# Two matrix products on one core, each done by seven half-sized block products in place of eight

## The chip, the cores and the metric

One core of one Trainium2 chip. The metric is the device time of the program in microseconds (us); lower is better. Executions of one kernel agree here to about 0.2%.

## The reference

```python
batch, m, k, h, n = 16, 512, 768, 3072, 768       # all inputs float32
y = np.matmul(x, w1) + b1                         # (8192 x 768) @ (768 x 3072)
y = 0.5 * y * (1.0 + erf(y / np.sqrt(2.0)))       # Gelu
return np.matmul(y, w2)                           # (8192 x 3072) @ (3072 x 768)
```

Both products have the same number of multiplications. I call them product one and product two.

## The kernel before

Everything is cast to fp16 by the loads. W1 and W2 stay in SBUF. Rows are taken in blocks of 512, and the scheduler orders the engines.

```python
for mb in range(n_mblk):                                  # 16 blocks of 512 rows
    gT = gtp.tile([P, HC, MB], F16, name="gT")
    for hc in range(HC):                                  # product one: 24 groups of 6 matmuls
        py = ps_y.tile([P, MB], FP32, ...)
        for kc in range(KC):
            nc.tensor.matmul(out=py[:], lhsT=w1b[:, kc, hc*P:(hc+1)*P], rhs=xT_cur[:, kc, :], ...)
        nc.scalar.activation(out=gT[:, hc, :], in_=py[:], func=Gelu, bias=b1t[:, hc:hc+1])
        # ... at hc == 12: the next block's x is transposed by DMA, the one after it is loaded
    for i in range(nsub):                                 # product two: 4 x 2 groups of 24 matmuls
        # ...
        for nb in range(2):
            for hc in range(HC):
                nc.tensor.matmul(out=pos[nb][:], lhsT=gT[:, hc, i*P:(i+1)*P],
                                 rhs=w2b[:, hc, nb*NB:(nb+1)*NB], ...)
            nc.vector.tensor_copy(out=osb[:, nb*NB:(nb+1)*NB], in_=pos[nb][:])
        nc.sync.dma_start(out=of[...], in_=osb[:])
```

Of the kernel before, what the change touches and what calls it, by code (L numbers as in the profile page):

```python
# [1 line left out]

# [5 lines left out]

FP32 = mybir.dt.float32  # L10
BF16 = mybir.dt.bfloat16
P = 128


@with_exitstack
def kernel(
    ctx: ExitStack,
    tc: tile.TileContext,
    x: bass.AP,
    w1: bass.AP,  # L20
    b1: bass.AP,
    w2: bass.AP,
    out: bass.AP,
):
    nc = tc.nc

    B, M, K = x.shape
    H = w1.shape[1]
    N = w2.shape[1]

    xf = x.rearrange("b m k -> (b m) k")
    of = out.rearrange("b m n -> (b m) n")
    R = B * M

    KC = K // P
    HC = H // P
    MB = 512
    NB = N // 2
    n_mblk = R // MB
    nsub = MB // P  # L40

    xr2 = x.rearrange("b (s p) k -> p (b s) k", p=P)
    w1r = w1.rearrange("(kc p) c -> p kc c", p=P)
    w2r = w2.rearrange("(hc p) n -> p hc n", p=P)

    F16 = mybir.dt.float16
    wpool = ctx.enter_context(tc.tile_pool(name="wpool", bufs=1))
    xbp = ctx.enter_context(tc.tile_pool(name="xbp", bufs=8))
    xtp = ctx.enter_context(tc.tile_pool(name="xtp", bufs=2))
    gtp = ctx.enter_context(tc.tile_pool(name="gtp", bufs=1))  # L50
    outp = ctx.enter_context(tc.tile_pool(name="outp", bufs=4))
    ps_y = ctx.enter_context(tc.tile_pool(name="ps_y", bufs=4, space=bass.MemoryType.PSUM))
    ps_o = ctx.enter_context(tc.tile_pool(name="ps_o", bufs=4, space=bass.MemoryType.PSUM))

    w1b = wpool.tile([P, KC, H], F16, name="w1b")
    w2b = wpool.tile([P, HC, N], F16, name="w2b")
    b1t = wpool.tile([P, HC], FP32, name="b1t")
    ident = wpool.tile([P, P], F16, name="ident")

    def load_x(mb):  # L60
        tiles = []
        for i in range(nsub):
            xh = xbp.tile([P, K], F16, name="xh")
            nc.gpsimd.dma_start(out=xh[:], in_=xr2[:, mb * nsub + i, :])  # L64
            tiles.append(xh)
        return tiles

    def transpose_by_dma(xhs):
        xT = xtp.tile([P, KC, MB], F16, name="xT")
        for i in range(nsub):  # L70
            nc.sync.dma_start_transpose(out=xT[:, :, i * P:(i + 1) * P], in_=xhs[i][:])
        return xT

    def transpose_by_pe(xhs):
        xT = xtp.tile([P, KC, MB], F16, name="xT")
        for i in range(nsub):
            pxt = ps_o.tile([P, KC, P], F16, space=bass.MemoryType.PSUM, name="po")
            for kc in range(KC):
                nc.tensor.transpose(out=pxt[:, kc, :], in_=xhs[i][:, kc * P:(kc + 1) * P],  # L79
                                    identity=ident[:])  # L80
            dst = xT[:, :, i * P:(i + 1) * P]
            if i % 2 == 0:
                nc.vector.tensor_copy(out=dst, in_=pxt[:])  # L83
            else:
                nc.scalar.copy(out=dst, in_=pxt[:])  # L85
        return xT

    make_identity(nc, ident[:])
    x0 = load_x(0)
    WG = 256  # L90
    for g in range(H // WG):
        c0 = g * WG
        nc.gpsimd.dma_start(out=w1b[:, :, c0:c0 + WG], in_=w1r[:, :, c0:c0 + WG])  # L93
        if g == 0:
            nc.sync.dma_start(out=b1t[:], in_=b1.rearrange("(hc p) -> hc p", p=P).rearrange("hc p -> p hc"))
    xT_cur = transpose_by_pe(x0)
    x_next = load_x(1)
    for g in range(HC // 3):
        nc.gpsimd.dma_start(out=w2b[:, 3 * g:3 * g + 3, :], in_=w2r[:, 3 * g:3 * g + 3, :])  # L99

    for mb in range(n_mblk):
        r0 = mb * MB
        gT = gtp.tile([P, HC, MB], F16, name="gT")
        xT_next = None
        for hc in range(HC):
            py = ps_y.tile([P, MB], FP32, space=bass.MemoryType.PSUM, name="py")
            for kc in range(KC):
                nc.tensor.matmul(out=py[:], lhsT=w1b[:, kc, hc * P:(hc + 1) * P],  # L108
                                 rhs=xT_cur[:, kc, :], start=(kc == 0), stop=(kc == KC - 1))
            nc.scalar.activation(out=gT[:, hc, :], in_=py[:],  # L110
                                 func=mybir.ActivationFunctionType.Gelu,
                                 bias=b1t[:, hc:hc + 1])
            if hc == 12 and mb + 1 < n_mblk:
                xT_next = transpose_by_dma(x_next)
                if mb + 2 < n_mblk:
                    x_next = load_x(mb + 2)
        for i in range(nsub):
            osb = outp.tile([P, N], FP32, name="osb")
            pos = [ps_o.tile([P, NB], FP32, space=bass.MemoryType.PSUM, name="po") for _ in range(2)]
            for nb in range(2):  # L120
                for hc in range(HC):
                    nc.tensor.matmul(out=pos[nb][:], lhsT=gT[:, hc, i * P:(i + 1) * P],  # L122
                                     rhs=w2b[:, hc, nb * NB:(nb + 1) * NB],
                                     start=(hc == 0), stop=(hc == HC - 1))
                nc.vector.tensor_copy(out=osb[:, nb * NB:(nb + 1) * NB], in_=pos[nb][:])  # L125
            nc.sync.dma_start(out=of[r0 + i * P:r0 + (i + 1) * P, :], in_=osb[:])
        xT_cur = xT_next


# [1 line left out]
_INS = ['x', 'w1', 'b1', 'w2']  # L131
_OUTS = [((16, 512, 768), 'float32')]


# [23 lines left out]
```

## Time and profile before

| | before |
|---|---|
| median time | 1034.11 us (1033.92 to 1035.1, 3 runs) |
| profiled span | 1033.5 us |
| TensorE (PE) busy | 1007.9 us |
| 128x512 matmuls, start to start | 2304 x 215.8 ns = 497 us |
| 128x384 matmuls, start to start | 3072 x 162.5 ns = 499 us |

These are lines of the page of the kernel before. First span and busy time by engine, then the clock that PE was granted in 40 slices (9 is full speed), then the chain of waits by engine, then the costliest groups: line, engine, operation, tiles and shape, count | busy us, mean ns | idle time before them and what ended it.

```profile
span 1033.5 us, 11849 instructions
PE 1007.9 (98%) x5400; PEld 530.0 (51%) x5400; DVE 72.5 (7%) x130; ACT 268.0 (26%) x388; POOL 50.7 (5%) x90
...
PEclk9969999999999999999999999999999999999999
...
PE 93%; DMA 5%; POOL 1%; issue 0%; DVE 0%; POOLq 0%
...
L122 PE MATMUL po<-w2b,gT 128*128 128x384 f16 x3072 | 507.5, 328 | 13.7 <-DMA w2b<-in_w_dram 13.7
L108 PE MATMUL py<-xT,w1b 128*128 128x512 f16 x2304 | 502.1, 380 | 1.2 <-DMA w1b<-in_w_dram 1.2
L110 ACT ACTIVATE gT<-py,b1t 128x512 f16<-128x512 f32 x384 | 263.8, 687 | 723.1 <-PE py L108 723.1
```

PE is on the chain for 93% and hardly waits; ACT and DVE are mostly idle. The mean of 380 ns in the groups is the length of one record; the records of matmuls overlap, so it is not the rate. The rate is read from the timeline, whose columns are start, duration, engine, line, operation and, in brackets, the idle time before:

```profile
27.87 0.69 ACT L110 ACTIVATE gT<-py,b1t 128x512 f16<-128x512 f32 x1 [0.61 <-PE py L108]
29.16 0.69 ACT L110 ACTIVATE gT<-py,b1t 128x512 f16<-128x512 f32 x1 [0.61 <-PE py L108]
...
504.00 0.56 DVE L125 COPY osb<-po 128x384 f32<-128x384 f32 x1 [34.42 <-PE po L122]
507.90 0.56 DVE L125 COPY osb<-po 128x384 f32<-128x384 f32 x1 [3.34 <-PE po L122]
```

Product one finishes a group of 6 matmuls every 1.295 us: 215.8 ns each. Product two finishes a group of 24 every 3.90 us: 162.5 ns each. All matmuls at that rate are 996.4 us. From the matmuls' starts in the trace, the rest of the 1033.5 us is: first real matmul at 11.2, matmuls at half clock 7.0, waits 14.7, end 4.2 us. Most of it falls into one window, in which PE also lost its clock while W2 arrived (columns: window, its length, busy us and count of each engine, granted clock, DMA share, GB/s):

```profile
core 0: us, PE busy (x) PEld busy (x) DVE busy (x) ACT busy (x) POOL busy (x), PEclk, DMA share, GB/s
44.50:80.00 35.50, 21.76 (x100) 11.00 (x99) 1.93 (x4) 0.69 (x1) 5.82 (x11) 0.71 1.20 189
```

### The profile page before, as it was taken

To read this page: it belongs to the slowest core of one execution; us is meant where nothing else is said; L and a number is where in the kernel's file an instruction comes from. 1 tells how busy PE (TensorE), PEld (TensorE's weight loads), DVE (VectorE), ACT (ScalarE), POOL (GpSimd) and SP (SyncE) were. 2 spreads that over 40 slices of the span, in tenths; PEclk is the share of its full clock that TensorE was granted. 3 is DMA by queue.
4 is the path that set the end of the run, shared out by engine and by line. 5 is a ranking of instruction groups with operands and counts; after the bars stand their busy time and mean duration, and the time that the engine had idled before them with its cause. 6 is when DMAs were issued, how large, how long until landed. Compare 5 with 4: busy or idle time off the path is not lost.

```text
span 1033.5 us, 11849 instructions
## 1 busy us (share of the span) xinstructions
PE 1007.9 (98%) x5400; PEld 530.0 (51%) x5400; DVE 72.5 (7%) x130; ACT 268.0 (26%) x388; POOL 50.7 (5%) x90
## 2 busy tenths in 40 slices
PE   6869999999999999999999999999999999999998
PEld 3335464554545455464554545555464554645554
DVE  0001010000101001010000101001010010101001
ACT  3401404123050331504224051330503214051230
POOL 5310000000000000000000000000000000000000
PEclk9969999999999999999999999999999999999999
DMA  9993040402305041050411404032050211100001
GB/s 164 202 184 91 10 98 16 92 31 33 85 6 92 31 65 58 2 105 16 77 47 24 84 16 92 31 51 72 1 107 16 47 46 17 61 16 31 31 3 59
DMA packets 82178, 59.77 MB, mean 58 GB/s; under 512 B 53456, under 2 KB 73936, under 8 KB 82128
## 3 DMA queue, kind: packets, MB, share of 16 engines
q0 software_dynamic: 21824, 22.03, 14.9%
q1 hardware_dynamic: 60304, 36.99, 13.5%
q8 instruction: 42, 0.69, 0.3%
q14 instruction: 8, 0.07, 0.0%
HBM read 44.05 MB, written 25.17 MB: 67 GB/s over the span
## 4 chain that ended last, share of the span: by engine, by line
PE 93%; DMA 5%; POOL 1%; issue 0%; DVE 0%; POOLq 0%
PE po L122 48%; PE py L108 45%; DMA w1b<-in_w_dram 3%; DMA w2b<-in_w_dram 3%; POOL w2b L99 0%; POOL w1b L93 0%; POOL xh L64 0%; DVE osb L125 0%; POOL ident masks.py:199 0%; POOL ident masks.py:197 0%; POOLq masks.py:199 0%; POOLq L142 0%
## 5 line engine op out<-in xcount | busy, mean ns | idle before, releaser
L122 PE MATMUL po<-w2b,gT 128*128 128x384 f16 x3072 | 507.5, 328 | 13.7 <-DMA w2b<-in_w_dram 13.7
L108 PE MATMUL py<-xT,w1b 128*128 128x512 f16 x2304 | 502.1, 380 | 1.2 <-DMA w1b<-in_w_dram 1.2
L110 ACT ACTIVATE gT<-py,b1t 128x512 f16<-128x512 f32 x384 | 263.8, 687 | 723.1 <-PE py L108 723.1
L122 PEld LDWEIGHTS <-gT 128*128 128x128 f16 x3072 | 301.9, 98 | 218.4 <-issue 20.2
L108 PEld LDWEIGHTS <-w1b 128*128 128x128 f16 x2304 | 225.9, 98 | 273.1 <-issue 3.0
L125 DVE COPY osb<-po 128x384 f32<-128x384 f32 x128 | 71.4, 558 | 949.1 <-PE po L122 949.1
L64 POOL DMA_DIRECT2D xh<-in_x_dram x64 | 34.1, 533 | 697.8 <-DMA xT<-xh 671.8
L93 POOL DMA_DIRECT2D w1b<-in_w_dram x12 | 9.9, 862 | 4.5 <-DMA w1b<-in_w_dram 4.5
L79 PE MATMUL po<-ident,xh 128*128 128x128 f16 x24 | 3.3, 310 | 6.7 <-DMA xh<-in_x_dram 6.5
L99 POOL DMA_DIRECT2D w2b<-in_w_dram x8 | 6.1, 761 | 6.4 <-DMA w1b<-in_w_dram 5.6
L79 PEld LDWEIGHTS <-xh 128*128 128x128 f16 x24 | 2.2, 138 | 7.5 <-DMA xh<-in_x_dram 7.5
L85 ACT COPY xT<-po 128x768 f16<-128x768 f16 x2 | 1.6, 798 | 7.2 <-PE po L79 7.2
L83 DVE COPY xT<-po 128x768 f16<-128x768 f16 x2 | 1.1, 558 | 8.6 <-PE po L79 8.6
L85 ACT ACT_TABLE_LOAD x1 | 1.3, 1283 | 0.7 <-PEq L142 0.7
L110 ACT ACT_TABLE_LOAD x1 | 1.3, 1283 | 0.0
masks.py:199 POOL TENSOR_SCALAR_AFFINE_SELECT ident<-ident 128x128 f16<-128x128 f16 x1 | 0.3, 305 | 0.1
masks.py:197 POOL MEMSET ident<- 128x128 f16 x1 | 0.2, 204 | 0.3 <-POOLq L142 0.3
L142 POOL MEMSET const-float32-0.0<- 128x1 f32 x1 | 0.1, 98 | 0.2 <-issue 0.2
L142 POOL MEMSET const-bfloat16-1.0<- 128x1 bf16 x1 | 0.1, 101 | 0.0
L142 POOL MEMSET const-uint8-127<- 128x1 uint8 x1 | 0.1, 101 | 0.0
L142 POOL MEMSET const-float32-1.0<- 128x1 f32 x1 | 0.1, 98 | 0.0
## 6 DMA issues: line engine op xcount, KB each, us to landing
out_dram<-osb SPq DMA_DIRECT2D x64, 384.0 KB, 2.3
xh<-in_x_dram POOLq DMA_DIRECT2D x64, 192.0 KB, 5.2
w1b<-in_w_dram POOLq DMA_DIRECT2D x12, 384.0 KB, 13.8
w2b<-in_w_dram POOLq DMA_DIRECT2D x8, 576.0 KB, 18.2
xT<-xh SPq DMA_TRANSPOSE x60, 4.1
b1t<-in_b_dram SPq DMA_DIRECT2D x1, 12.0 KB, 5.7
```

The source lines that it names most:

```text
L64: nc.gpsimd.dma_start(out=xh[:], in_=xr2[:, mb * nsub + i, :])
L79: nc.tensor.transpose(out=pxt[:, kc, :], in_=xhs[i][:, kc * P:(kc + 1) * P], identity=ident[:])
L83: nc.vector.tensor_copy(out=dst, in_=pxt[:])
L85: nc.scalar.copy(out=dst, in_=pxt[:])
L93: nc.gpsimd.dma_start(out=w1b[:, :, c0:c0 + WG], in_=w1r[:, :, c0:c0 + WG])
L99: nc.gpsimd.dma_start(out=w2b[:, 3 * g:3 * g + 3, :], in_=w2r[:, 3 * g:3 * g + 3, :])
L108: nc.tensor.matmul(out=py[:], lhsT=w1b[:, kc, hc * P:(hc + 1) * P], rhs=xT_cur[:, kc, :], start=(kc == 0), stop=(kc == KC - 1))
L110: nc.scalar.activation(out=gT[:, hc, :], in_=py[:], func=mybir.ActivationFunctionType.Gelu, bias=b1t[:, hc:hc + 1])
L122: nc.tensor.matmul(out=pos[nb][:], lhsT=gT[:, hc, i * P:(i + 1) * P], rhs=w2b[:, hc, nb * NB:(nb + 1) * NB], start=(hc == 0), stop=(hc == ...
L125: nc.vector.tensor_copy(out=osb[:, nb * NB:(nb + 1) * NB], in_=pos[nb][:])
L142: nc = _bacc.Bacc("TRN2", target_bir_lowering=False, num_devices=1)
```

## The change

A product of matrices cut into 2 x 2 blocks needs eight block products; with sums made beforehand and afterwards it needs seven (Strassen's scheme in Winograd's form). The change does this to both products, on row blocks of 1024:

- Per block, product one has 12 units of 7 x 3 matmuls of 128x512, product two 4 units of 7 x 12 matmuls of 128x384. In all 96 x 21 = 2016 and 32 x 84 = 2688 matmuls, 7/8 of before.
- DVE makes the sums of x, W1, Gelu output (G) and W2 in fp16.
- The sums of products are grown in PSUM (the accumulator memory that PE writes, used here as banks bX, bY, bZ, bW): ACT or DVE copies a partial result to a second bank, and PE goes on adding to both.
- The sums need SBUF, so W1 no longer stays there: every block loads it again, one unit at a time, 192 loads in all.
- The order on each engine is written by hand: unit i starts while unit j = i - 1 ends.

The core of the diff (the whole old loop goes out; cuts are marked):

```diff
-        for hc in range(HC):
-            # ... 6 matmuls into py, Gelu, as above
-        for i in range(nsub):
-            # ... 2 x 24 matmuls into po, copies, store
+B11, B21, T1, B22, T3, T2, T4 = range(7)          # slots of a weight tile: 4 loaded, 3 sums
+        def load_wt(n):                           # W1 for one unit, again in every block
+            for half in range(2):
+                nc.gpsimd.dma_start(out=wt[:, 2*half:2*half+2, :, :]..., in_=w1r[:, :, c0:c0+P])
+        def t_ops(o, n, q, q4=None):              # DVE sums of weights, in place
+            later(n, lambda: tt(o(T3), o(B22), o(T1), SUB), q)
+            later(n, lambda: tt(o(T1), o(T1), o(B11), SUB), q)
+            later(n, lambda: tt(o(T2), o(B22), o(T1), SUB), q)
+            later(n, lambda: tt(o(T4), o(B21), o(T2), SUB), q if q4 is None else q4)
+        # ... sums of x (XS) and of G (GS) alike
+        def period(i, j, fill):                   # not at the turn from product one to two:
+            p1(i); copy_xy(i)                     # PE into bX;      ACT copies bX to bY
+            p7(j); add_c22(j)                     # PE adds to bY;   DVE: bY + pw to SBUF
+            fill(1)                               # waiting DVE sums are placed in the fills
+            p5(i); copy_w(i)                      # PE into bW;      ACT copies bW to pw
+            p3(j); add_c12(j)                     # PE adds to bZ;   DVE: bZ + pw, then ACT Gelu of 1024
+            p6(i); copy_yz(i)                     # PE adds to bY;   DVE copies bY to bZ
+            p4(j)                                 # PE adds to bY;   ACT Gelu of 512
+            p2(i)                                 # PE adds to bX;   ACT Gelu of 512
+        # ... at the turn p1(i) is spread between p7(j), p3(j), p4(j)
+        # ... start: 8 x tiles loaded and transposed on PE, then x_sums(), prep_wt(0)
+        for g, (kind, sb, k) in enumerate(units):
+            # ... fill(): prep_wt, prep_w2, g_sum, loads, by unit and slot
+            cur = Unit1(g, sb, k) if kind == 1 else Unit2(g, sb, k)
+            period(cur, prev, fill)
+            prev = cur
```

## The prediction

> **What bounds it now.** TensorE. The busy table gives PE 1007.9 of 1033.5 us; the chain of waits is 93% PE; ACT is at 26%. In the timeline the first product's Gelus come every 1.295 us, one per 6 matmuls: 215.8 ns per 128x512 matmul. The second product's copies come every 3.90 us, one per 24: 162.5 ns per 128x384 matmul. 2304 and 3072 of them make 497 + 499 = 996 us. The other 37 us are the start (first real matmul at 11.2 us), the w2 waits (PE waited 13.7 us for DMA; granted clock 0.71 between 44.5 and 80 us), and 3.5 us at the end.
>
> **What changes.** 96 units x 21 = 2016 matmuls of 128x512 and 32 x 84 = 2688 of 128x384. At the spacings above 435 + 437 = 872 us: 124 us less, all on the critical path. Widths and weight loads per matmul stay, so I expect the same spacings.
>
> Added, meant to be hidden:
> - ACT in product one, per unit of 21 x 0.2158 = 4.53 us: two 512 PSUM copies (estimate 0.58 each, from 798 ns for 768), two Gelus of 0.687, one 1024 Gelu (1.11): 3.6 us, 80%. The Trainium skill, "ScalarE: Activation LUTs", What ACT_TABLE_LOAD costs, gives 280 ns + 0.833 ns per element for an ACTIVATE with a pointer bias: 707 for 512, where the trace shows 687.
> - DVE per unit: three fp32 512 operations of 0.69 us (Trainium skill, "VectorE: DVE Perf Modes", the errata section: (N+151)/0.96 ns; the trace's 384 copy, 558 ns, agrees) and four fp16 sums of 384 (about 0.3): 3.3 us, 72%, plus sums of G and, in block 0, W2.
> - The tight loop is a latency: third product, DVE add, 1024 Gelu, two Gelus, copy, sixth product. Laid out by hand with 0.2 us per hop it arrives within 0.2 us of PE's need: up to 0.2 us of stall per unit, say 10 us over 96.
> - Product-two units (13.65 us) leave ACT and DVE mostly idle; sixteen turns cost perhaps 0.5 us each: 8 us.
> - DMA: W1 eight times, in 192 loads of 768 packets half as long as before. Before, 768 longer packets took 2.0 us. So at most 4 us per unit, 32 us for the eight units that must load during a 54 us product-one phase: hidden, except block 0, where 16 W2 loads compete: 4 us.
> - Start: eight x tiles, transposes, four x sums (0.9 each) and weight sums stand before the fifth product: PE continues near 22 us, cold for a few us: 24 us in all (the w2 waits mostly go). End: 4 us.
>
> **Sum.** 872 + 24 + 4 + 10 + 8 + 4 = 922; some stalls overlap, so 917 us. Range 898 to 946. Faster by over 2%: 0.97; within 2%: 0.02; slower: 0.01.
>
> **What would show it.** About 4760 matmuls; product-one units every 4.5 to 4.7 us, product-two units every 13.7; PE above 90% of the chain; ACT busy about 430 us, DVE about 400; DMA 100 to 140 GB/s with PE waiting little on wt; granted clock above 0.97.
>
> **What would make it wrong.** Product one may be latency-bound through ACT and DVE: units of 5 us or more add 45 us (PE's waits would name the ACT copy into bY, or DVE). W1 loads with 256-byte destination runs may cost over 4 us each: then PE waits for wt, 100 us or more. A cold start or late W2 costs 10 to 20. Below 905 only if stalls are nearly nil.

## The result

| | before | after |
|---|---|---|
| median time | 1034.22 us (4 runs) | 906.46 us (906.21 to 907.44, 4 runs) |
| ratio | | 0.8765, 95% interval 0.875 to 0.878 |
| profiled span | 1033.5 us | 904.5 us |

A ratio is the mean time of one kernel's fast runs over that of the other's of the same rounds, so it is not quite the ratio of the medians quoted. The values of the changed kernel were found correct.

These are lines of the page of the kernel after, with the DMA queue that takes most (packets, MB, share of the 16 engines' span):

```profile
span 904.5 us, 12591 instructions
PE 886.6 (98%) x4764; PEld 465.6 (51%) x4764; DVE 529.0 (58%) x1045; ACT 386.2 (43%) x614; POOL 204.9 (23%) x278
...
PEclk7999999999999999999999999999999999999999
...
q0 software_dynamic: 166144, 55.07, 56.1%
...
PE 92%; DMA 5%; DVE 1%; POOL 1%; issue 1%; ACT 0%; DVEq 0%; POOLq 0%
...
L111 POOL DMA_DIRECT2D wt<-in_w_dram x192 | 158.0, 837 | 489.3 <-PE bY_92 L192 344.4
L207 ACT ACTIVATE G_78<-tmp,b1t 128x1024 f16<-128x1024 f32 x96 | 110.2, 1148 | 123.8 <-DVE tmp L276 123.8
```

PE has 636 fewer matmuls and the same 98%. DVE went from 72.5 to 529.0 us of work and ACT from 268.0 to 386.2, and the chain still runs along PE for 92%. POOL spends 158.0 us on sending the 192 W1 loads, and what it waits for there is mostly PE (344.4 of 489.3 us), which has to free a tile first: outside block 0 the loads run ahead of the need. The Gelu of 1024 lasts 1148 ns, where I had put 1.11 us. This is what PE waited for in the kernel after (total us, times, longest):

```profile
PE bW L192 <- DVE wt L86: 4.0, 1, 4.0
PE bT_96 L151 <- DMA xh<-in_x_dram: 3.7, 3, 2.6
PE bY_92 L192 <- DVE bZ L287: 1.7, 4, 0.7
PE bY_93 L192 <- DVE bZ L287: 1.5, 4, 0.5
```

These are few, and nearly all lie in the first 80 us. An account of both spans, from the matmuls' starts in the trace (each interval less 215.8 or 162.5 ns; the surplus is called half clock where the matmul itself was long, and a wait otherwise):

| us | before | after | difference |
|---|---|---|---|
| first real matmul at | 11.2 | 15.6 | +4.4 |
| matmuls at full rate | 996.4 | 871.9 | -124.5 |
| half clock after that | 7.0 | 2.3 | -4.7 |
| PE waits after that | 14.7 | 10.3 | -4.4 |
| after the last matmul began | 4.2 | 4.4 | +0.2 |
| span | 1033.5 | 904.5 | -129.0 |

So the gain is the matmul count, and the rest nearly cancels: the change begins 4.4 us later and has 10.3 us of waits of its own, while the waits for W2 and the half clock that followed them are gone. The 10.3 us of waits are 4.2 before the fifth product p5 of the first unit, 5.0 in the rest of block 0, and 1.1 later: 0.11 at each of seven turns from product one to two, and 0.4 at one place in block 3. Otherwise PE does not wait in blocks 1 to 7.

Why the crowded period does not stall is seen in its timeline. This is one period of the kernel after in block 2, PE, ACT and DVE lines of the longest loop:

```profile
254.23 0.81 PE L192 MATMUL bZ<-XS_87,wt 128*128 128x512 f16 x3
...
254.46 1.13 DVE L86 TENSOR_TENSOR wt<-wt 128x384 f16<-128x384 f16 x3
...
255.51 0.68 DVE L276 TENSOR_TENSOR tmp<-bZ,pw 128x512 f32<-128x512 f32 x1
...
256.23 1.15 ACT L207 ACTIVATE G_78<-tmp,b1t 128x1024 f16<-128x1024 f32 x1 [1.21 <-DVE tmp L276]
...
257.28 0.67 ACT L212 ACTIVATE G_77<-bY_93,b1t 128x512 f16<-128x512 f32 x1
...
257.85 0.68 ACT L212 ACTIVATE G_77<-bX_90,b1t 128x512 f16<-128x512 f32 x1
...
258.42 0.59 ACT L256 COPY bY_93<-bX_91 128x512 f32<-128x512 f32 x1
...
259.41 0.81 PE L192 MATMUL bY_93<-XS_85,wt 128*128 128x512 f16 x3
```

The third product, p3, begins at 254.23, DVE is at sums of W1 until then and adds from 255.51, then ACT runs four instructions in a row, and the sixth product, p6, which needs the last of them, begins at 259.41. That copy ends at 258.42 + 0.59 = 259.01: 0.4 us to spare. On ACT the starts are 1.05, 0.57 and 0.57 us apart, although the records last 1.15, 0.67 and 0.68: each instruction starts about 0.1 us before the one ahead of it ends. Three such overlaps are 0.3 us.

In block 0 it is different. The same kernel, DVE and PE lines ahead of one of the stalls:

```profile
46.84 1.15 DVE L86 TENSOR_TENSOR wt<-wt 128x384 f16<-128x384 f16 x3 [0.94 <-DMA wt<-in_w_dram]
...
47.91 0.68 DVE L276 TENSOR_TENSOR tmp<-bZ,pw 128x512 f32<-128x512 f32 x1
...
48.69 0.70 DVE L287 COPY bZ<-bY_93 128x512 f32<-128x512 f32 x1
...
49.45 0.81 PE L192 MATMUL bY_93<-XS_86,wt 128*128 128x512 f16 x3 [0.39 <-DVE bZ L287]
```

DVE works in order. It waits 0.94 us for a W1 tile, so its next add is late, so its copy to bZ is late, and PE waits for that copy before p7. But DVE is also crowded there by the sums of W2, and either may be the cause. The DMA share in windows of the kernel after points to the loads: 1.52 in a window of block 0, where W1 and W2 are loaded at once, against 0.78 in product one of block 1.

```profile
core 0: us, PE busy (x) PEld busy (x) DVE busy (x) ACT busy (x) POOL busy (x), PEclk, DMA share, GB/s
...
45.00:62.00 17.00, 15.99 (x72) 6.85 (x71) 14.74 (x31) 11.59 (x19) 10.47 (x14) 1.00 1.52 194
140.00:195.00 55.00, 55.00 (x263) 25.53 (x262) 40.57 (x92) 38.62 (x59) 16.34 (x22) 1.00 0.78 88
```

(The share can pass 1: the records of packets overlap in time.)

### The profile page after: what moved, and what is told of

Its sections match the earlier page's. It is cut to its first block, busy times and chain, and to the rows that moved or that the text cites. A ratio compares the mean times of both kernels' runs of the same rounds, so it can differ in the third digit from the quotient of the medians.

```text
span 904.5 us, 12591 instructions
## 1 busy us (share of the span) xinstructions
PE 886.6 (98%) x4764; PEld 465.6 (51%) x4764; DVE 529.0 (58%) x1045; ACT 386.2 (43%) x614; POOL 204.9 (23%) x278
## 3 DMA queue, kind: packets, MB, share of 16 engines
q0 software_dynamic: 166144, 55.07, 56.1%
## 4 chain that ended last, share of the span: by engine, by line
PE 92%; DMA 5%; DVE 1%; POOL 1%; issue 1%; ACT 0%; DVEq 0%; POOLq 0%
PE bY_93 L230 10%; PE bY_92 L230 10%; PE bY_93 L192 9%; PE bY_92 L192 9%; PE bX_90 L230 7%; PE bZ L230 7%; PE bX_91 L230 7%; PE bW L230 7%; PE bW L192 6%; PE bZ L192 6%; PE bX_91 L192 6%; PE bX_90 L192 6%; DMA wt<-in_w_dram 3%; DMA xh<-in_x_dram 1%; DVE wt L86 1%
## 5 line engine op out<-in xcount | busy, mean ns | idle before, releaser
L192 PEld LDWEIGHTS <-wt 128*128 128x128 f16 x2016 | 197.6, 98 | 245.2 <-issue 11.2
L111 POOL DMA_DIRECT2D wt<-in_w_dram x192 | 158.0, 837 | 489.3 <-PE bY_92 L192 344.4
L207 ACT ACTIVATE G_78<-tmp,b1t 128x1024 f16<-128x1024 f32 x96 | 110.2, 1148 | 123.8 <-DVE tmp L276 123.8
L86 DVE TENSOR_TENSOR wt<-wt 128x384 f16<-128x384 f16 x384 | 135.6, 353 | 10.2 <-DMA wt<-in_w_dram 3.3
L270 ACT COPY pw<-bW 128x512 f32<-128x512 f32 (+1 forms) x128 | 71.8, 561 | 112.2 <-PE bW L230 88.4
L230 PEld LDWEIGHTS <-G_78 128*128 128x128 f16 x768 | 75.2, 98 | 50.4
L192 PE MATMUL bW<-XS_84,wt 128*128 128x512 f16 x288 | 78.5, 382 | 4.0 <-DVE wt L86 4.0
L192 PE MATMUL bX_90<-XT,wt 128*128 128x512 f16 x288 | 78.9, 383 | 0.0
L192 PE MATMUL bX_91<-XT,wt 128*128 128x512 f16 x288 | 77.8, 379 | 0.0
L192 PE MATMUL bZ<-XS_87,wt 128*128 128x512 f16 x288 | 77.8, 379 | 0.0
L230 PE MATMUL bW<-w2o,GS_79 128*128 128x384 f16 x384 | 67.6, 326 | 0.0
L287 DVE COPY bZ<-bY_92 128x512 f32<-128x512 f32 (+1 forms) x64 | 42.6, 666 | 17.3 <-PE bY_92 L230 11.2
L230 PEld LDWEIGHTS <-G_77 128*128 128x128 f16 x384 | 37.6, 98 | 27.4
L230 PEld LDWEIGHTS <-GS_81 128*128 128x128 f16 x384 | 37.6, 98 | 25.6
L230 PEld LDWEIGHTS <-GS_82 128*128 128x128 f16 x384 | 37.6, 98 | 25.6
L230 PEld LDWEIGHTS <-GS_80 128*128 128x128 f16 x384 | 37.6, 98 | 24.8
```

The source lines that it names most:

```text
L86: nc.vector.tensor_tensor(out=o, in0=a, in1=b, op=op)
L111: nc.gpsimd.dma_start(out=wt[:, 2 * half:2 * half + 2, :, :].rearrange("p a k c -> p (a k) c"), in_=w1r[:, :, c0:c0 + P])
L192: nc.tensor.matmul(out=dst[:, 0:RH], lhsT=self.wt[:, slot, c, :], rhs=a[:, c, :], start=first and c == 0, stop=c == self.C - 1, skip_group ...
L207: nc.scalar.activation(out=G2[:, hi, :, :], in_=self.tmp[:], func=GELU, bias=b1t[:, NH + hi:NH + hi + 1])
L230: nc.tensor.matmul(out=dst[:, 0:N2], lhsT=a, rhs=w2o[:, slot, c, :], start=first and c == 0, stop=c == self.C - 1, skip_group_check=True)
L270: nc.scalar.copy(out=u.pw[:, 0:u.F], in_=bW[:, 0:u.F])
```

## Experiments

Each kernel is the changed one with the edit shown; edits are shortened, and lines in words stand for longer code. They ran in three jobs on three chips; the kernel before had a median of 1034.93 us (experiments 1, 2, 4, 5), 1034.64 us (6, 7, 8, 10) and 1034.59 us (3, 9, 11) in them, so times of different jobs may be compared to about 1 us. "Waits" are PE's waits from the account above; a profile is one execution.

### 1 and 2: one product alone by seven

```diff
 one_by_seven: product two
-    per unit 7 products of 12 matmuls, sums of G and W2
+    per unit 4 groups of 24 matmuls on G1, G2 and the loaded quarters of W2, then copies
 two_by_seven: product one
-    per unit 7 products of 3 matmuls, sums of x and W1
+    per unit 4 groups of 6 matmuls on x and the loaded quarters of W1, then Gelus
```

> Only the first product keeps the seven products; the second is done by eight (3072 matmuls of 128x384, no sums of G or W2). Theory A (the gain is the matmul count alone, all added work is hidden): 435 + 499 + about 33 of start, end and block 0, so 965 to 970 us, 62 us above the changed kernel; block 0 loses its stalls, so it may be 4 less. Theory B (the added sums and copies of a product eat part of its gain): the second product's saving would be below 62, so this kernel would stand less than 55 us above the changed one.

> Only the second product keeps the seven products; the first is done by eight (2304 matmuls of 128x512, four plain Gelus per unit, no sums of x or W1; W1 is still reloaded per block). Theory A (matmul count alone): 497 + 437 + the overheads; the start should lose about 5 us since no sums stand before the matmuls, so 960 to 967 us. Theory B (ACT and DVE in the first product cost something): this kernel would stand less than 50 us above the changed one, since removing the crowded work would pay for part of the added matmuls.

Measured: 971.25 us (ratio 0.9385) with product one alone by seven, and 956.95 us (0.9245) with product two alone. The first gave wrong values, for which see 3; its matmul count and order are as meant, and its time stands.

The first lies just above the 965 to 970 expected, the second 3 us below its 960 to 967.

Product two by seven is worth 971.25 - 906.46 = 64.8 us, where 384 matmuls x 0.1625 are 62.4: all of it, and theory B for product two (less than 55 us) falls. The 2.4 us more belong to the kernel of the experiment: after block 0 its PE waits 3.8 us in all where the changed one's waits 1.1. One thing was not as expected: it has no sums of W2 and none of G, and DVE is busy for 38.5 of the 60 us from 20 to 80 where it was 50.0, and still PE waits 4.2 us in block 0 after 25 us. This counts in 7 to 9. Product one by seven is worth 956.95 - 906.46 = 50.5 us, where 288 x 0.2158 are 62.2: it loses 11.7. The account says where. In the kernel with product two alone by seven the first real matmul comes at 15.5 us, half clock costs 1.4, and after it PE does not wait over 0.04 us at any matmul. Its chain of waits is PE to 98%:

```profile
PE 98%; DMA 1%; POOL 0%; issue 0%; ACT 0%; POOLq 0%
```

So the 10.3 us of waits of the changed kernel and 0.9 us more of half clock are the price of the seven products in product one, all but 1.1 us of it paid at the start and in block 0. Theory A (the matmul count alone) holds for product two. For product one it holds in the later blocks, not at the start and in block 0. Theory B (removing the crowded work pays for part of the added matmuls) set its bound at less than 50 us, and 50.5 lies at that bound; but it meant a steady cost of ACT and DVE, and of that the account shows nothing.

### 3: the wrong values

```diff
 one_by_seven_fixed
-                    bank = (bX, bY)[row][half]
+                    bank = (bX[0], bX[1], bW)[(4 * u + 2 * row + half) % 3]
```

> The kernel with only the first product by seven gave wrong values (relative error 0.11). My reason: its plain second product opened accumulation groups of 384 columns in the banks bY, which clears the bank's accumulate marks and sets them for 384 columns only; the next first-product unit then adds into columns 384 to 511 of data that ACT put there, and the matmul overwrites instead. Here the plain groups use only bX and bW, which every unit opens anew. Expected: correct, and the same time, 970 to 972 us.

Measured: correct, 976.09 us (2 runs). The Trainium skill, "PSUM — Partial Sum Buffer", The four PSUM rules, says that a group's first matmul clears the marks of its whole bank, that a matmul without that flag adds where the mark is set and overwrites where it is not, and that ACT and DVE writes leave the marks alone. This run agrees: moving the plain groups out of the banks that the scheme adds to made the values right. (It does not tell this reason from another fault in the use of those banks.) That is also why the changed kernel may copy into bY and bZ and add to them: after its warm-up matmuls of full width it opens no group in these banks. The time missed my figure by 4 us through my edit: with three banks, PE waited 4.0 us in all for ACT to empty one.

### 4 and 5: how much room ACT's loop has

```diff
             u.left_done(0, bX[u.g % 2])
+            if isinstance(u, Unit1):
+                nc.scalar.copy(out=spare[:, 0:cols], in_=u.pw[:, 0:cols])   # 8 or 512 columns
```

> One more ACT copy of 128x8 per product-one unit, behind the second Gelu and ahead of the next copy from bX to bY, about 0.2 us. In the changed kernel's trace that copy ends at 31.40 us and the matmul that needs it starts at 31.79: about 0.35 us to spare per unit. Theory A (the loop has that slack): no change, 906 to 908 us. Theory B (the loop is what sets the 4.53 us period, as my prediction half assumed): plus 0.2 x 96 = 19 us.

> The same with a copy of 128x512, about 0.61 us. ACT would be busy 4.27 of 4.53 us per unit, still below full. Theory A (a latency loop with 0.35 us of slack): plus 0.25 to 0.3 us in the eleven later units of each of eight blocks, 22 to 27 us, so 928 to 934 us, with the waits of PE naming the ACT copy into bY. Theory C (only ACT's capacity counts): no change, 906 to 910 us.

Measured: 906.73 us with the small copy and 913.59 us with the big one. The small copy's record lasts 0.19 us, but the next copy starts 0.09 us after it (253.47 and 253.56), so it adds 0.09 us to the loop and theory B would ask for about 9 us. It is free, so the loop does not set the period: theory B falls. The big one costs 7 us, less than the 22 to 27 expected but not nothing, so ACT's capacity alone (theory C) does not decide either. The profile of the kernel with the big copy shows the loop reaching PE:

```profile
255.65 0.61 ACT L295 COPY spare<-pw 128x512 f32<-128x512 f32 x1
...
256.16 0.59 ACT L257 COPY bY<-bX 128x512 f32<-128x512 f32 x1
...
256.80 0.81 PE L193 MATMUL bY<-XS,wt 128*128 128x512 f16 x3
```

The extra copy takes 256.16 - 255.65 = 0.51 us of ACT's time, not the 0.61 of its record, again by the overlap, and p6 begins 0.05 us after the copy that it needs has ended. PE's waits after block 0 rose from 1.1 to 8.1 us. They are not spread evenly: there are 42 of them, six in each of seven blocks, mostly 0.17 us and mostly in every second unit. 0.51 us of added work less 0.17 is about 0.35 us of slack, the expected figure (in the timeline above, 0.40 from the copy's end to p6, less the 0.05 that p6 follows it by here). That only every second unit waits follows, as I read it, from the order on PE: p3, which begins the loop, stands before the p6 that waits, so a wait gives the next loop that much more time. So the 22 to 27 us were missed because the copy added 0.51 and not 0.61 us, and because nearly half of the units pay nothing.

### 6: W1 in packets of half the size

```diff
 w1_half_rows
-            nc.gpsimd.dma_start(out=wt[:, 2*half:2*half+2, :, :]..., in_=w1r[:, :, c0:c0+P])
+            for h0 in (0, P // 2):
+                nc.gpsimd.dma_start(out=wt[..., h0:h0+P//2]..., in_=w1r[:, :, c0+h0:c0+h0+P//2])
```

> Each W1 load in two halves of 64 columns: twice the packets, each of 128 bytes written, the same bytes; the software queue issues four loads per unit at about 0.83 us. If a packet has a fixed cost (from the records: 41 ns for 256 bytes written, 60 for 512, 79 for 768, 135 for 1536: 22 ns plus 19 per 256), it takes about 31 ns, the W1 traffic costs up to 1.5 times the engine time of now, and it stays hidden in blocks 1 to 7; block 0, where loads already come late, gains 5 to 15 us of stall: 910 to 922 us. If the packets' cost is by bytes alone: no change.

Measured: 911.17 us (ratio 0.881). A packet of 128 bytes written lasted 32 ns in the median, where the line gave 31. The queue of these loads took 78.4% of the engines' span against 56.1%. PE's waits in block 0 after 25 us rose from 5.0 to 8.8 us; in all later blocks together they rose by 0.8. So blocks 1 to 7 have room for the added W1 time, and block 0 has none. The records of packets overlap, so their sum overstates it: by the landings of the loads in block 0, one unit's W1 took the queue about 2.6 us where it took 2.2.

### 7 to 9: what stalls block 0

```diff
 w2_late
-            in block 0's product one: T3 = B22 - T1; T1 = T1 - B11; T2 = B22 - T1; in product two: T4
+            in block 0's product one: T1 = T1 - B11; T2 = B22 - T1; in product two: T3 = T2 - B11; T4
 w2_early
-                        for q, c in w2_loads[:2]:
+                        for q, c in w2_loads[:8 if k == 0 else 2]:
 w2_both: w2_late, and w2_early with 10 for 8
```

> Block 0 has eight stalls of PE of 0.5 to 0.9 us, on the copy from bY to bZ on DVE. Here two of the four sums of W2 are put off until product two: 6 us less DVE work in block 0's product one, the loads untouched. Theory D (DVE has too much work in block 0): the stalls fall from 5 us to under 2, so 3 to 4 us faster. Theory E (the DMA queues are full, W1 tiles come late and DVE waits in order): stalls stay, within 1 us of the changed kernel.

> The other way: eight of the sixteen W2 loads go out in the first unit, where the DMA queues are idle, instead of two; DVE's work untouched. Theory D (DVE overloaded): stalls stay at 4 to 5 us. Theory E (W1 tiles late): the waits of DVE for the W1 loads vanish and the stalls with them, 3 to 4 us faster.

> Block 0 alone, both cures: ten of the W2 loads go out in the first unit, and two of the four W2 sums are put off to product two. Theory E (late W1 tiles stall DVE, which then gives bZ late) with DVE's load second: the stalls of PE in block 0 after the start fall from 5 us to under 1.5; 902 to 904 us. If the stalls stay above 3 us, neither the loads nor the sums are their cause.

> The changed kernel as it is, to stand beside the next ones on the same chip: 906 to 907 us, with about 5 us of PE stalls in block 0 after the start.

| | median us | PE waits in block 0 after 25 us |
|---|---|---|
| after, and again | 906.46, 907.42 | 5.0, 4.5 |
| w2_late | 906.33 | 4.9 |
| w2_early | 904.72 | 3.1 |
| w2_both | 906.74 | 4.8 |

The changed kernel again gave 907.42 us, as expected to 0.4 us. The edit of w2_late is smaller than its text says: T4 was put off already before it, so it takes four sums, 2.6 us of DVE's 50.0 busy between 20 and 80 us, out of product one and not 6. With this much less work for DVE, PE waits as long. In the profile of w2_late:

```profile
46.80 1.14 DVE L86 TENSOR_TENSOR wt<-wt 128x384 f16<-128x384 f16 x3 [1.46 <-DMA wt<-in_w_dram]
...
48.65 0.70 DVE L292 COPY bZ<-bY 128x512 f32<-128x512 f32 x1
...
49.40 0.81 PE L197 MATMUL bY<-XS,wt 128*128 128x512 f16 x3 [0.90 <-DVE bZ L292]
```

DVE's wait for W1 is 1.46 us where it was 0.94, and what stands behind it comes at the same time as before. Theory D (DVE overloaded) falls, more by the kernel of experiment 1, which has no sums of W2 and 11.5 us less DVE work there and waits nearly as long, than by this edit. Of theory E one half holds: W1 comes late, and DVE waits for it in order. The other half, that sending W2 out earlier cures it, held for eight loads (about 2 us; the ratio's interval, 0.8732 to 0.8758, just touches the changed kernel's, so the waits carry this) and failed for ten. By its expectation's own rule, 4.8 us of stalls would clear the loads as well. The trace says otherwise: the stalls of w2_both are others. With the ten W2 loads ahead of it, unit 4's W1 landed at 39.53 us where it had landed at 34.79, DVE waited 2.36 us for it, and PE stood for 1.87 us before the p7 behind it; this and the next unit's wait of 0.75 are more than half of the 4.8.

Both kinds of load go out on one queue, and it sets the pace of block 0. Per unit it carries two W1 and two W2 loads. In the trace of the kernel after they land one behind the other, W1 about 1.1 us apart and W2 1.45: 5.1 us for a unit's four, and from 43 to 70 us the second W2 load of each unit lands 5.1 us after that of the unit before. The stalled units come every 5.1 us as well (p7 at 44.29, 49.45 and 54.51), in place of 4.53. POOL sends the four in 3.2 us, so the sending is not what limits them. The list of DMA issues shows the delay, in a window of block 0 and in product one of block 1 (count, KB, median us from issue to landing):

```profile
wt<-in_w_dram POOLq DMA_DIRECT2D x10, 192.0 KB, 8.1
...
wt<-in_w_dram POOLq DMA_DIRECT2D x16, 192.0 KB, 4.0
```

Two other kernels agree. With W1 in half-size packets (experiment 6) a unit's loads land 5.5 us after those of the unit before, once 6.6, and the stalled units keep the same distance. The kernel with product two alone by seven sends the same loads in the same order, they too land 5.1 us after those of the unit before, its units last 24 x 0.2158 = 5.2 us, and PE waits nowhere. So while W2 is on its way, block 0 asks for more time of the queue than a unit has. Eight loads sent early gained because the queue stood empty from 24.4 to 29.0 us in the changed kernel. W2 loads spread thinner, behind W1, might gain more. No thinner order was run, so what it is worth is open, and so is what inside the DMA sets the 5.1 us.

### 10 and 11: the start, and everything together

```diff
 start
-        load 4 x tiles, W1 unit 0, 4 x tiles, W1 units 1 to 3; x_sums(); prep_wt(0)
+        load 8 x tiles, W1 units 0 to 3; sums in the order XS0, T3, T1, XS1, T2, XS2, XS3, T4
+                    if not j:
+                        p2(i)                    # first unit: behind p1, since it needs no sums
 best2: start, w2_both, the sums of unit 1 mixed in by need, and at the turn
+                p1(i, 0, 3)
                 p7(j)
```

> The start alone: all eight x tiles are loaded ahead of W1, the second product p2 of the first unit (which needs no sums) goes behind p1, and the sums are made in the order in which the products need them. The fifth product started at 21.0 us. Expected near 17.5, with PE less idle before it: 3 to 4 us faster, 902 to 904 us. If the x loads are not what the start waits for: 2 us or less.

> All together: the early start, the DVE sums of units 0 and 1 in the order of need (the start alone still left a gap of 2.4 us before p7 of the first unit, and a cold clock after it), both cures for block 0, and three matmuls of the next unit ahead of p7 at the turn. 872 us of matmuls, about 14 us of start, 4 of end, 2 of stalls: 893 to 897 us.

The start alone: 902.14 us (901.55 to 903.03; ratio 0.872, interval 0.8707 to 0.8733, clear of the 0.875 to 0.878 of the changed kernel). The first real matmul came at 13.8 instead of 15.6 us, p5 at 16.5 instead of 21.0. A wait of 2.2 us in front of p7 of the first unit was left, since DVE made the other sums first:

```profile
20.86 0.81 PE L192 MATMUL bY<-XS,wt 128*128 128x512 f16 x3 [2.20 <-DVE bZ L287]
```

All together: 906.04 us, 4 us worse than the start alone, and outside the 893 to 897 expected. That long wait before p7 was gone, and so were the seven later turns' waits, but PE stood still for 5.5 us before unit 4 and then ran at half clock:

```profile
37.99 1.46 PE L197 MATMUL bX<-XT,wt 128*128 128x512 f16 x3 [5.47 <-DMA wt<-in_w_dram]
```

Ten W2 loads stood in the queue ahead of unit 4's W1, and PE, which had started earlier, wanted that tile earlier; after that it waited 2.2 us more for a copy on DVE, which stood behind that unit's sums. Waiting for W1 in block 0 took back all that the better start had won. The start alone is the best kernel that ran, 0.5% below the changed one.

## Why the prediction was right or wrong

The time, 906.46 us, lies in the predicted range of 898 to 946, 10.5 us under the predicted 917. Point by point:

- **What bounds it, and the worth of the fewer matmuls: right.** 872 us were predicted, 871.9 found; the spacings of 215.8 and 162.5 ns did not change. Experiment 1 confirms product two's half to 2.4 us.
- **ACT's loop, "up to 0.2 us of stall per unit", 10 us: the largest mis-sized term; it was nil.** What I took for 0.2 us late came 0.4 us early. The whole 0.6 us cannot be traced. The trace shows two parts: the three overlaps on ACT give back 0.3 us, and the hop from DVE to ACT took 0.04 us (256.19 to 256.23) where 0.2 was allowed. Against that, DVE began its add 0.47 us after p3's record ended. Experiments 4 and 5 confirm the slack and that it is a latency loop. The Trainium skill, "ScalarE: Activation LUTs", What ACT_TABLE_LOAD costs, has the missing number in the same paragraph as the formula that I used: back-to-back ACTIVATEs overlap by about 93 ns. The trace agrees, with 0.1 us.
- **Turns, sixteen at 0.5 us, 8 us: mis-sized; 0.8 us** at seven turns from product one to two after block 0 (0.11 each), nothing in the other direction.
- **The start, 24 us: right in sum;** 15.6 + 4.2 + 2.3 = 22.1 us, with the fifth product at 21.0 for "near 22".
- **Block 0, "16 W2 loads compete: 4 us": right;** 5.0 us, by way of DVE, which waits for W1 in order. That the loads compete was foreseen; the 4 us has no working, so its size is partly luck.
- **W1 traffic hidden otherwise: right.** The list of PE's waits names no W1 load. The fear of costly short packets was not borne out: 41 ns each.
- **The end: right,** 4.4 us for 4.
- **Busy times: off.** ACT 386 us for 430, DVE 529 for 400. 96 units at the predicted 3.3 us are 317 of it, which leaves 83 for the rest, where the sums of G alone took 137, and a weight sum took 0.353 us for the 0.3. It did not matter, since neither is on the chain.

The predicted 917 was 10.5 us too high mainly by the loop's 10 and the turns' 8, less the 5 us taken off for overlap. In sum 871.9 + 22.1 + 4.4 + 0.8 + 5.0 + 0.4 (one place in block 3) = 904.6 for a span of 904.5, where the prediction had 922 before it allowed for overlap.

## What to carry to other kernels

When added work on idle engines can reach the chain only through a latency loop, lay the loop out with start-to-start times and not with the durations of single records: here 0.1 us per instruction on ACT was half of the difference between the stall foreseen and the slack found. When matmuls are the whole chain, fewer of them are worth their spacing, and the loss is to be looked for at the start, where no earlier work hides the sums and loads. Compare what a shared queue needs per unit with what the unit lasts: here 5.1 us against 4.53, and PE took the queue's pace. Before sending a load out early on such a queue, ask which load then comes late.

## What the Trainium skill lacked or had wrong

- "DMA: Bandwidth & Descriptors", Specifications, gives 512 bytes as the least transfer for line rate, with read-modify-write below. In these loads, which cast fp32 to fp16, no step is seen there: packets of 1536, 768, 512, 256 and 128 bytes written last 135, 79, 60, 41 and 32 ns in the median, a line of about 22 ns and 19 ns for each 256 bytes written. (Only the last is under 512 bytes on the fp32 side too. Records overlap, so these are not rates: by landings in block 0 the queue wrote about 203, 179 and 156 GB/s with packets of 768, 256 and 128 bytes.)
- "ScalarE: Activation LUTs", What ACT_TABLE_LOAD costs, states the overlap for ACTIVATEs; here it holds as well between a Gelu and a copy (starts 0.57 us apart, record 0.68) and between two copies (0.51 apart, record 0.61).
- "VectorE: DVE Perf Modes", the errata section, gives (N + 151)/0.96 ns for an fp32 add and does not say where the operands lie; with one operand in PSUM and N = 512 that is 691 ns, and the records of 684 to 691 ns agree. A copy of 512 from one PSUM bank to another took 699.
